# Second branch product of a hybrid encoder block as seven half products, with its sums formed earlier

## The chip, the cores and the metric

The kernel runs on one core of a Trainium2 chip. The metric is device time in microseconds (us); the time before is a median of three runs. All arithmetic is fp32: a product of two fp32 matrices is made of three TensorE matmuls on high and low parts (high x high, high x low, low x high), which the code calls fp32r parts.

## The reference

One encoder block on x of 1024 tokens by 1024 channels:

```
h = rms_norm(x);  proj = h @ w_in      (q, k, v, r, gate codes, attention q/k/v, two branch gates)
A = gated linear attention(proj) @ w_o_gla        (branch A)
B = windowed attention(proj)     @ w_o_swa        (branch B)
x = x + (sigmoid(gate_a) * A + sigmoid(gate_b) * B) @ w_out
x = x + (silu(h2 @ w_g) * (h2 @ w_u)) @ w_ffn_out,   h2 = rms_norm(x)
```

The change is about `B`'s projection, a product of a 1024 x 1024 weight (`w_ob` in the kernel) with the attention's output.

## The kernel before

Activations stand transposed: channels on the 128 partitions, tokens along the free dimension in two halves of 512 (`HT`). The stages follow each other on TensorE:

1. the first projections and the norm (0 to about 40 us);
2. the linear attention, 46 slots (loop over `t`, L649 to L656). Each slot issues pieces of the linear attention and, between them, a share of the dense projections' matmuls (`fill`, table `GF`). Behind each slot one step of `x_sums` (L606) runs: a load of a tile of x, or a difference of two such tiles that is stored to DRAM, for the later pair products. These tiles come from the pool `xn`, three buffers of 128 x 512;
3. the windowed attention, 22 slots (L865 to L880), filled in the same way from the dense projections. Head outputs are stored to DRAM by `a_out` (L820), one store for each of four heads, 64 KB each;
4. the other halves of three projections as pairs (`pair_*`, to about 720 us);
5. branch A's projection by `seven` (L1123);
6. branch B's projection by `both` (L1096);
7. `w_out` by `seven` again, then the feed-forward part.

`seven` multiplies 2 x 2 blocks with seven half products in place of eight. The row tiles of the weight are taken as pairs (k, k + 4), the contraction as its two halves, the tokens as two halves. The half products are named "11", "21", "T1", "T2", "T3", "T4", "22"; the T products take sums of weight blocks (formed by VectorE when needed, `comb` and `sub`) and differences of operand blocks. Each is done for four k, each time 4 blocks x 3 matmuls of 128 x 512 (`product`, L910). `both` does the plain product: for each of 8 row tiles `m`, two weight units of 4 blocks, and 6 matmuls a block (two token halves, three part products).

A weight tile is loaded (`rawload`, `wunit`), its high part copied by ScalarE and its low part subtracted by VectorE (`wsplit`, L890), into pools of five buffers each (`wh`, `wl`). Operand tiles are split in the same way into named sets (`xset`, sets S0 to S6, each with four high and four low tiles). A gate is loaded from DRAM, put through a sigmoid on ScalarE, and multiplied with the product and added by VectorE (L1269, L1270). `merge` (L1188) then forms the operands of the `w_out` product.

Order: TensorE's order is the written one (`manual_schedule`). For the other engines a scheduler fixes the order at compile time by program priority and a timing model; `tc.keep_in_program_order` and `tc.issue_after` pin single instructions. All DMA transfers are issued by SyncE, in order: one that waits for a buffer or for data holds up those behind it. On-chip memory is given out in pools stacked on each other; when a group of pools is closed (`glas.close()` L657, `swas.close()` L881), a pool that is laid over one of them waits for that pool's last use. The pools `swc` and `swt` hold the windowed attention; `tp` and `bo`, which follow, lie over `swt` (`tp` holds the tiles t2h, t2l, np, nt; `bo` the sets S0 to S3, used from about 600 us on), and `wq` (wr2, ws) lies over `swc` alone.

## Time and profile before

| | |
|---|---|
| median of three runs | 1606.47 us (1606.43 to 1606.72) |
| profiled execution | 1607.29 us, span 1605.5 us, granted TensorE clock 1.00 |
| TensorE matmul busy | 1596.9 us, 7532 matmuls |
| VectorE / ScalarE busy | 1209.1 us / 903.5 us |
| DMA | 323.24 MB, mean 201 GB/s |

A page of the profile gives the busy time of each engine (PE is TensorE, PEld its weight loads, DVE VectorE, ACT ScalarE, SP SyncE, SPq SyncE's queue), the chain of work that ended last, groups of instructions (line, engine, operation, output <- inputs with buffer numbers left out, then busy us, mean ns of one, idle us before them and what ended it), and the DMA issues (KB each, median us to landing). Stretches give the busy time of each engine between two times. Matmuls are pipelined, so their listed lengths overlap; the distance between starts is what counts. A line number can be a helper's.

### The profile page before, as it was taken

What the parts mean: (1) busy time and instruction counts of PE and PEld (TensorE: products, weight loads), DVE (VectorE), ACT (ScalarE), POOL (GpSimd) and SP (SyncE); (2) the same over time, 40 slices, a digit from 0 to 9 for tenths busy, and PEclk for the clock granted to TensorE, in tenths of its full rate; (3) what the DMA queues carried; (4) which work ended last, traced back from release to release, by engine and by line L of the source; (5) the groups of instructions that cost most, each with busy time, mean ns of one, the idle gap of its engine ahead of it and who ended that gap; (6) DMA issues with size and microseconds to landing.
All of it is one profiled execution on the core that took longest, in us unless ns stands there. A gap on an engine that the chain in (4) does not pass through costs nothing.

```text
span 1605.5 us, 23093 instructions
## 1 busy us (share of the span) xinstructions
PE 1596.9 (99%) x7532; PEld 1330.1 (83%) x7532; DVE 1209.1 (75%) x2287; ACT 903.5 (56%) x1859; POOL 0.2 (0%) x4
## 2 busy tenths in 40 slices
PE   9999999999999999999999999999999999999999
PEld 6888888888888788888888888888888888888887
DVE  8568888746999678786855877777777878689655
ACT  7456778755998645455633656844444444354442
POOL 0000000000000000000000000000000000000000
PEclk9999999999999999999999999999999999999999
DMA  8856767888544487868733656634344564695433
GB/s 270 301 196 213 248 216 259 285 264 286 173 145 139 152 291 246 273 228 273 243 124 105 220 186 204 202 114 151 112 145 157 191 202 161 207 330 175 151 99 118
DMA packets 197979, 323.24 MB, mean 201 GB/s; under 512 B 23423, under 2 KB 49919, under 8 KB 197858
## 3 DMA queue, kind: packets, MB, share of 16 engines
q1 hardware_dynamic: 197858, 321.77, 60.8%
q8 instruction: 59, 0.97, 0.2%
q14 instruction: 62, 0.51, 0.1%
HBM read 216.29 MB, written 105.39 MB: 200 GB/s over the span
## 4 chain that ended last, share of the span: by engine, by line
PE 95%; DVE 2%; ACT 1%; DMA 1%; issue 0%; SPq 0%; DVEq 0%; ACTq 0%
PE mm L73 22%; PE mm L916 10%; PE mm L915 10%; PE mm L914 10%; PE ch L73 8%; PE mm L1458 7%; PE ch L1458 6%; PE ch L914 5%; PE ch L916 5%; PE ch L915 5%; PE mm L246 4%; PE ch L813 1%; PE ch L585 0%; PE ch L756 0%; PE ch L490 0%
## 5 line engine op out<-in xcount | busy, mean ns | idle before, releaser
L893 ACT ACTIVATE wh<-ws 128x512 fp32r<-128x512 f32 x164 | 103.2, 630 | 157.4 <-PE mm L915 83.8
L73 PE MATMUL mm<-wh,xl 128*128 128x512 f32 x320 | 127.3, 398 | 0.0
L73 PE MATMUL mm<-wh,xh 128*128 128x512 f32 x320 | 126.9, 397 | 0.3 <-ACT lrt L313 0.3
L73 PE MATMUL mm<-wl,xh 128*128 128x512 f32 x320 | 127.1, 397 | 0.0
L894 DVE TENSOR_TENSOR wl<-ws,wh 128x512 fp32r<-128x512 f32 x164 | 112.2, 686 | 15.8 <-ACT wh L893 15.4
L67 ACT ACTIVATE wh<-wr 128x512 fp32r<-128x512 f32 x114 | 71.1, 630 | 55.2 <-issue 16.9
L69 DVE TENSOR_TENSOR wl<-wr,wh 128x512 fp32r<-128x512 f32 x114 | 77.9, 686 | 22.0 <-ACT wh L67 20.5
L893 ACT ACTIVATE wh<-a 128x512 fp32r<-128x512 f32 x66 | 41.6, 632 | 90.3 <-PE mm L1458 42.7
L893 ACT ACTIVATE wh<-wr 128x512 fp32r<-128x512 f32 x76 | 47.9, 631 | 60.9 <-PE mm L915 20.2
L894 DVE TENSOR_TENSOR wl<-a,wh 128x512 fp32r<-128x512 f32 x66 | 45.5, 690 | 40.4 <-ACT wh L893 40.2
L73 PEld LDWEIGHTS mm<-wh,xh 128*128 128x128 f32 x320 | 60.3, 188 | 10.6 <-ACT lrt L313 0.8
L1458 PE MATMUL mm<-hl,wh 128*128 128x512 f32 x176 | 68.6, 390 | 0.0
L1458 PE MATMUL mm<-hh,wl 128*128 128x512 f32 x176 | 68.6, 390 | 0.0
L1458 PE MATMUL mm<-hh,wh 128*128 128x512 f32 x176 | 68.5, 389 | 0.0
L73 PEld LDWEIGHTS mm<-wl,xh 128*128 128x128 f32 x320 | 60.3, 188 | 9.6
L73 PEld LDWEIGHTS mm<-wh,xl 128*128 128x128 f32 x320 | 60.3, 188 | 9.0
L907 DVE TENSOR_TENSOR ws<-wr,wr 128x512 f32<-128x512 f32 x80 | 54.5, 686 | 8.0 <-DMA wr<-in_w_f_dram 4.0
L894 DVE TENSOR_TENSOR wl<-wr,wh 128x512 fp32r<-128x512 f32 x76 | 51.9, 684 | 7.6 <-ACT wh L893 7.0
L1425 DVE TENSOR_TENSOR hl<-hr,hh 128x512 fp32r<-128x512 f32 x77 | 52.8, 686 | 5.1 <-ACT hh L1424 5.1
L1424 ACT ACTIVATE hh<-hr 128x512 fp32r<-128x512 f32 x77 | 47.6, 619 | 7.9 <-DMA hr<-B 4.1
L1458 PE MATMUL ch<-hh,wh 128*128 128x512 f32 x132 | 51.4, 389 | 0.0
L1458 PE MATMUL ch<-hh,wl 128*128 128x512 f32 x132 | 51.4, 389 | 0.0
(449 smaller groups left out, 4910.1 us busy)
## 6 DMA issues: line engine op xcount, KB each, us to landing
wr<-in_w_fi_dram SPq DMA_DIRECT2D x110, 256.0 KB, 4.0
wr<-in_w_f_dram SPq DMA_DIRECT2D x96, 256.0 KB, 3.7
wh<-wh SPq DMA_DIRECT2D x80, 256.0 KB, 3.3
wl<-wl SPq DMA_DIRECT2D x80, 256.0 KB, 3.1
B<-c SPq DMA_DIRECT2D x44, 256.0 KB, 2.1
T<-st SPq DMA_DIRECT2D x44, 256.0 KB, 3.1
a<-in_w_fo_dram SPq DMA_DIRECT2D x44, 256.0 KB, 5.1
hr<-T SPq DMA_DIRECT2D x44, 256.0 KB, 2.7
```

Source lines behind the costliest of these rows:

```text
L67: nc.scalar.activation(h, raw, AF.Copy)
L69: nc.vector.tensor_tensor(l, raw, h.bitcast(F32), op=ALU.subtract)
L73: nc.tensor.matmul(o, a, b, start=start, stop=stop)
L246: nc.tensor.matmul(Y[q], w[:, c], x, start=f0, stop=f1, skip_group_check=True)
L893: nc.scalar.activation(h, src, AF.Copy)
L894: nc.vector.tensor_tensor(l, src, h.bitcast(F32), op=ALU.subtract)
L907: nc.vector.tensor_tensor(t, x, y, op=op)
L914: nc.tensor.matmul(o, h[:, c], x[kk][0], start=start and kk == 0, stop=False, skip_group_check=True)
L915: nc.tensor.matmul(o, h[:, c], x[kk][1], start=False, stop=False, skip_group_check=True)
L916: nc.tensor.matmul(o, l[:, c], x[kk][0], start=False, stop=kk == nk - 1, skip_group_check=True)
L1425: nc.vector.tensor_tensor(l, r, h.bitcast(F32), op=ALU.subtract)
L1458: nc.tensor.matmul(ys[m], a[:, c], b, start=f0, stop=f1, skip_group_check=True)
```

## The change

- `both`, `prep_b` and `merge` go. Branch B's product is done by a new function `branch_b` with the same seven half products as `seven`, for the first time with branch B's operands and weights. Its results are added to the sum in five gated parts (`gated_by`), 20 in all.
- The operand sums (T1 to T4) of branch B are formed by `b_sums(n)`, called behind the last four slots of the windowed attention. It loads four blocks from DRAM, takes four differences and stores them. It uses the two buffers of `qr`. The head outputs go into grouped DRAM tiles with one store of 256 KB for four heads.
- The weight sums for T1, T2 and T3, and the ready-made high and low parts of the sum for "22", are formed by `w_sums` behind `x_sums` in the linear attention (24 more steps; slots 2 to 13 take two steps), and stored. So are the parts of `w_out`'s first four weight tiles, which the next `seven` then reads (`first`).
- While branch A's product runs, three operand sets of four tiles are loaded and split (`bset`) in place of four such sets; the other four sets follow during `branch_b`. The operands of the `w_out` product are formed in the last steps of `branch_b` and the first of `seven` (`m_T1`, `m_rest`).

```
+        def w_sums():
...
+            def form(key, d, x, y, op):
+                tc.keep_in_program_order(nc.vector.tensor_tensor(d, x, y, op=op))
+                if key:
+                    put(key, d)
+
+            def parts(key, d):
+                h, l = (gtile(t, (P, 512), FR, bufs=1) for t in ("pwh", "pwl"))
+                nc.scalar.activation(h, d, AF.Copy)
+                tc.keep_in_program_order(nc.vector.tensor_tensor(l, d, h.bitcast(F32), op=ALU.subtract))
+                for n, v in (("h", h), ("l", l)):
+                    put((key[0] + n, key[1]), v.bitcast(F32))
+
+            w = i["w_ob"]
+            for k in range(4):
+                a, c, b = load(w[k, 0]), load(w[k + 4, 1]), load(w[k + 4, 0])
+                form(("bs1", k), c, b, c, ALU.add)
+                yield
+                form(("bs3", k), b, a, b, ALU.subtract)
+                yield
+                form(("bs2", k), c, c, a, ALU.subtract)
+                yield
+                d = load(w[k, 1])
+                form(None, d, d, c, ALU.subtract)
+                yield
+                parts(("bs4", k), d)
+                yield
+                parts(("wo", k), load(i["w_out"][k, 0]))
+                yield
...
-                if t:
+                for _ in range(2 if 2 <= t <= 13 else t > 0):
                     next(sums, None)
...
-            for h in range(4):
-                nc.sync.dma_start(out=scr["b", 4 * g + h, n // 4][:, (n % 4) * P:(n % 4 + 1) * P],
-                                  in_=ob[:, h])
+            nc.sync.dma_start(out=heads(f"b{g + 1}{n // 4 + 1}", n), in_=ob)
+
+        def b_sums(n):
+            x1, x2 = (sw.tile([P, 8, P], F32, tag="qr", name=nm("qr")) for _ in range(2))
+            a, b, c, d = x1[:, 0:4], x1[:, 4:8], x2[:, 0:4], x2[:, 4:8]
+            for q, v in (("b11", a), ("b12", b), ("b22", c), ("b21", d)):
+                nc.sync.dma_start(out=v, in_=heads(q, n))
+            for q, t, x, y in (("bT1", b, b, a), ("bT2", c, c, b), ("bT3", a, c, a), ("bT4", d, d, c)):
+                nc.vector.tensor_tensor(t, x, y, op=ALU.subtract)
+                nc.sync.dma_start(out=heads(q, n), in_=t)
...
+                    b_sums(t - 2 * KT - 2)
...
+        def parted(key, k):
+            r = []
+            for n in "hl":
+                t = wp.tile([P, 512], FR, tag="w" + n, name=nm("w" + n), bufs=5)
+                nc.sync.dma_start(out=t.bitcast(F32), in_=scr[key + n, k])
+                r.append(t)
+            return r
...
+        def gated_by(d, v, m, s):
+            turns[0] += 1
+            g = bt.tile([P, HT], F32, tag=("ga", "gb")[turns[0] % 2], name=nm("gb"))
+            nc.sync.dma_start(out=g, in_=scr[f"gb{m}", s])
+            nc.scalar.activation(g, g, AF.Sigmoid)
+            nc.vector.tensor_tensor(g, v, g, op=ALU.mult)
+            nc.vector.tensor_tensor(d, g, d, op=ALU.add)
+
+        def branch_b(w, S, mid):
...
+            for k in K:
+                Y[k] = mmtile()
+                product(Y[k], load(w[k, 0]), S["11"], 4, True, True)
+                X[k] = chtile((P, HT))
+                nc.scalar.copy(X[k], Y[k])
+                after("11", k)
+            for k in K:
+                product(Y[k], load(w[k, 1]), S["21"], 4, False, True)
+                gated_by(xg[k][0], Y[k], k, 0)
+                after("21", k)
+            for k in K:
+                Z[k] = mmtile()
+                product(Z[k], load(scr["bs1", k]), S["T1"], 4, True, False)
+                p5[k] = bo.tile([P, HT], F32, tag=f"S3h{k}", name=nm("p5"))
+                nc.scalar.copy(p5[k], Z[k])
+                after("T1", k)
+            for k in K:
+                product(X[k], load(scr["bs2", k]), S["T2"], 4, False, True)
+                gated_by(xg[k][1], X[k], k, 1)
+                after("T2", k)
+            for k in K:
+                product(X[k], load(scr["bs3", k]), S["T3"], 4, False, True)
+                nc.vector.tensor_tensor(p5[k], X[k], p5[k], op=ALU.add)
+                gated_by(xg[k + 4][1], p5[k], k + 4, 1)
+                after("T3", k)
+            for k in K:
+                product(X[k], load(w[k + 4, 1]), S["T4"], 4, False, True)
+                gated_by(xg[k + 4][0], X[k], k + 4, 0)
+                after("T4", k)
+            for k in K:
+                product(Z[k], parted("bs4", k), S["22"], 4, False, True)
+                gated_by(xg[k][1], Z[k], k, 1)
+                after("22", k)
...
-                   2: (lambda k: prep_b(0, k), lambda k: prep_b(1, k)), 3: (lambda k: prep_b(2, k),),
-                   6: (lambda k: prep_b(3, k),)}, hl)
+                   2: (bset("11"),), 3: (bset("21"),), 6: (bset("T1"),)}, hl)
+            branch_b(i["w_ob"], BX, {"11": (bset("T2"),), "21": (bset("T3"),),
+                                     "T1": (bset("T4"), lambda k: yset("11", k, xg[k][0])), "T2": (bset("22"),),
+                                     "T4": (lambda k: yset("21", k, xg[k + 4][0]),), "22": (m_T1,)})
...
-            for m in (0, 4, 1, 5, 2, 6, 3, 7):
-                g = [gate(f"gb{m}", s) for s in range(2)]
-                y = both(i["w_ob"], m, ob)
-                for s in range(2):
-                    nc.vector.tensor_tensor(g[s], y[s], g[s], op=ALU.mult)
-                    nc.vector.tensor_tensor(xg[m][s], g[s], xg[m][s], op=ALU.add)
-                if m > 3:
-                    merge(m - 4)
...
-                  {0: (lambda k: yset("T3", k, xg[k][0]), lambda k: yset("22", k, xg[k + 4][1])),
-                   1: (lambda k: yset("T2", k, xg[k][1]),),
+                  {0: (m_rest,), 1: (lambda k: yset("T2", k, xg[k][1]), lambda k: yset("T3", k, xg[k + 4][1])),
...
+                  None, lambda k: parted("wo", k))
```

`bset(q)` loads the four tiles of an operand set from DRAM and splits them into a set of S0 to S6; `first` in `seven` replaces the split weight of its first half product.

More of the change, by code (lines that the diff above doesn't have):

```diff
@@ L1145, in seven @@
                 Y[k] = mmtile()
-                product(Y[k], wsplit(held(k, k, 0), 512), S["11"], 4, True, True)
+                product(Y[k], first(k) if first else wsplit(held(k, k, 0), 512), S["11"], 4, True, True)
                 X[k] = chtile((P, HT))
@@ L1186, in seven, with load, after @@
                 after(6, k)
-        def merge(k):
+        turns = [0]
+        def gated_by(d, v, m, s):
[6 more added lines that the diff above has]
+        def branch_b(w, S, mid):
+            K = range(4)
+            n = [0]
+            def load(src):
+                n[0] += 1
+                return wsplit(rawload(src, n[0] % 2), 512)
+            def after(q, k):
+                for f in mid.get(q, ()):
+                    f(k)
+            Y, X, Z, p5 = ([None] * 4 for _ in range(4))
+            for k in K:
[31 more added lines that the diff above has]
+                after("22", k)
```

68 lines of the change are left out of this document (34 added, 34 removed).

## The prediction

> **What bounds the kernel now.** I read the page first: the busy shares and the chain that ended last.
>
> ```profile
> span 1605.5 us, 23093 instructions
> ...
> PE 1596.9 (99%) x7532; PEld 1330.1 (83%) x7532; DVE 1209.1 (75%) x2287; ACT 903.5 (56%) x1859; POOL 0.2 (0%) x4
> ...
> PE 95%; DVE 2%; ACT 1%; DMA 1%; issue 0%; SPq 0%; DVEq 0%; ACTq 0%
> ```
>
> TensorE carries the end: 95% of the chain, and 8.6 us without work in the whole span (1605.5 - 1596.9). A removed matmul is worth its full length wherever the other engines keep up. Next I took the chain in order of time (start, length, what), for the stage that changes and its neighbours:
>
> ```profile
> 352.57 20.21 PE mm L73 x89
> ...
> 554.62 14.53 PE mm L246 x64
> ...
> 808.77 87.04 PE mm L73 x384
> ```
>
> The last row is the second branch product: 384 matmuls without a break in 87.04 us, so 87.04 / 384 = 0.2267 us each. Last, the busy times by stretches, to see which engine has room where the change puts new work:
>
> ```profile
> core 0: us, PE busy (x) PEld busy (x) DVE busy (x) ACT busy (x) POOL busy (x), PEclk, DMA share, GB/s
> 70.00:150.00 80.00, 80.00 (x427) 68.60 (x427) 57.80 (x118) 41.70 (x97) 0.00 (x0) 1.00 0.63 211
> 230.00:300.00 70.00, 69.61 (x408) 60.44 (x408) 61.68 (x149) 57.65 (x163) 0.00 (x0) 1.00 0.78 259
> 300.00:350.00 50.00, 49.38 (x263) 41.16 (x264) 24.06 (x65) 34.76 (x104) 0.00 (x0) 1.00 0.83 276
> 370.00:380.00 10.00, 10.00 (x49) 8.26 (x48) 3.68 (x10) 1.87 (x5) 0.00 (x0) 1.00 1.03 373
> 380.00:520.00 140.00, 139.32 (x758) 120.09 (x757) 132.54 (x381) 127.60 (x313) 0.00 (x0) 1.00 0.54 169
> 528.00:555.00 27.00, 25.92 (x134) 20.60 (x133) 16.30 (x42) 18.18 (x45) 0.00 (x0) 1.00 0.38 127
> 540.00:550.00 10.00, 9.02 (x46) 6.68 (x45) 5.17 (x13) 7.92 (x20) 0.00 (x0) 1.00 0.38 116
> 809.00:896.00 87.00, 87.00 (x385) 72.07 (x385) 51.63 (x83) 33.85 (x59) 0.00 (x0) 1.00 0.37 113
> 896.00:985.00 89.00, 89.00 (x395) 73.66 (x394) 72.77 (x117) 51.50 (x89) 0.00 (x0) 1.00 0.66 211
> ```
>
> From 555 to the end TensorE never waits in the product stages. It loses about a microsecond at the attention's end (25.92 of 27) and about one around the end of the linear attention (0.39 and 0.62). Those two places are where the change adds work.
>
> **The product (a term of the sum).** Before: 8 output tiles x 2 weight units x 4 blocks x 6 matmuls = 384. After: 7 half products x 4 row tiles x 4 blocks x 3 matmuls = 336. The 48 that go, of the same shape, are 48 x 0.2267 = 10.88 us off the path; the stage becomes 76.2 us.
>
> **Does VectorE keep up there?** I counted the instructions in the new stage: 24 subtractions for weight low parts, 40 for the gates (20 gatings of a product and an addition), 16 for the splits of four operands, 4 additions of the held product, 12 splits for the next product and 4 differences: 100 on VectorE, and 24 + 20 + 8 + 16 + 12 = 80 on ScalarE.
>
> ```profile
> L1269 DVE TENSOR_TENSOR gb<-mm,gb 128x512 f32<-128x512 f32 x15 | 9.7, 686 | 26.7 <-PE mm L73 26.7
> L67 ACT ACTIVATE wh<-wr 128x512 fp32r<-128x512 f32 x14 | 8.6, 623 | 20.7 <-issue 16.9 <-PE mm L73 3.7
> L837 DVE TENSOR_TENSOR S4l<-xg,S4h 128x512 fp32r<-128x512 f32 x4 | 2.8, 688 | 0.0
> ```
>
> ```profile
> 360.30 0.68 DVE L679 TENSOR_TENSOR qA<-cosb,qg 128x512 f32<-128x512 f32 x1
> 360.90 0.69 DVE L680 SCALAR_TENSOR_TENSOR qB<-sinb,qg 128x512 f32<-128x512 f32 x1
> 361.51 0.69 DVE L681 TENSOR_TENSOR qB<-sinb,qg 128x512 f32<-128x512 f32 x1
> ```
>
> In these groups of the stage (busy, mean ns, then idle before) one VectorE instruction of 512 columns takes 0.686 us, but in the row of three from the timeline each starts 0.60 us after the last: their ends overlap. So 100 are 60 to 69 us, and 80 on ScalarE at 0.623 are 50 us, both inside 76.2. Step by step, a product gives TensorE 12 x 0.2267 = 2.72 us, and the fullest steps hold four VectorE instructions: 2.4 to 2.75 us. The last four products and the first four of the next stage read ready-made weight parts and cost VectorE none. The stage at 896 to 985 is nearly this one (seven half products, gates replaced by residuals): VectorE 72.77 of 89, TensorE 89.00 of 89. No gain beyond the matmuls is possible, since TensorE waits nowhere here. I take 0, with 0 to 1 us as bounds; the cover is the five weight buffers, prepared up to four products (10.9 us) ahead.
>
> The stage before it splits 12 operands instead of 16, so it gets lighter. Transfers in the new stage: 24 weights, 8 parts, 20 gates, 16 operands of 256 KB, 17.8 MB in 76 us or 234 GB/s, against 259 and more in stretches where TensorE is full. Nothing.
>
> **Sums of weights in the linear attention.** 24 steps are added behind the 32 that exist, and slots 2 to 13 now take two. Each new step has one VectorE instruction, 8 have a ScalarE copy, and together they issue 20 loads and 28 stores of 256 KB. The existing steps, by the view of their tile (min/median/max ns, first and last start), the last output of the linear attention, by the timeline, and two rows of transfers (KB, median us to landing):
>
> ```profile
> L603 DVE TENSOR_TENSOR xn<-xn,xn x16: 682/685/689, 78.0 to 303.3; 128x512 f32<-128x512 f32 x16
> ```
>
> ```profile
> 352.61 0.37 ACT L587 COPY ot<-ch 128x256 f32<-128x256 f32 x1 [1.01 <-PE ch L585]
> ```
>
> ```profile
> xT<-xn SPq DMA_DIRECT2D x16, 256.0 KB, 2.8
> qr<-sq SPq DMA_DIRECT2D x16, 256.0 KB, 3.2
> ```
>
> The third old step ran at 78.0 and the last, slot 32, at 303.3; the last slots end near 352.6. Doubling in slots 2 to 13 falls roughly into 70 to 150, where VectorE has 57.8 of 80: 12 x 0.6 us fit. Slots 21 to 32 only exchange one step for another; VectorE is at 88% there (61.68 of 70) and gets no instruction more. Slots 33 to 44 get 12 new VectorE instructions in 46 us where it is half idle (24.06 of 50). What is tight there is the transfers: 24 x 256 KB = 6.3 MB in 46 us is 137 GB/s on top of 276, together 413, and the highest rate of any stretch I read is 373. (413 - 373) x 46 us = 1.8 MB, or 4.9 us, would be left over. All transfers go through SyncE's queue in order, so the dense projections' weights stand behind the new loads, and the new loads wait for one of three staging buffers.
>
> ```profile
> SPq L170 <- PE mm L73: 23.1, 18, 3.9
> ```
>
> The wait of that queue for TensorE (23.1 us in 18 waits) says that the re-read weights are fetched as early as the five buffers allow, up to 10.9 us of matmuls ahead of use. That covers a lag of 4.9 us for weights; the short backward chain of the linear attention has less cover. Bounds 0 and 4.9 us; I take 1, near the 0.62 already lost in that stretch.
>
> **Operand sums at the attention's end.** Four rounds, one a slot, each four loads, four dependent subtractions, four stores; 16 VectorE instructions x 0.6 = 9.6 us, of which 528 to 555 leaves 10.7 free (16.30 of 27). On SyncE the 64 stores of the attention's outputs become 16, against 32 issues more in the rounds. The rounds borrow the two query buffers, and the memory of the whole attention is handed to the next stage at its last use. The timeline shows such a hand-over, and the tile view of np (us to landing) and its copy what follows it:
>
> ```profile
> 357.21 0.69 DVE L678 TENSOR_TENSOR kA<-cosb,kg 128x512 f32<-128x512 f32 x1 [7.48 <-DMA o<-ot]
> ...
> 528.95 0.60 PE L756 MATMUL ch<-ident,qr 128*128 128x128 f32 x4
> ...
> 555.14 0.64 ACT L836 ACTIVATE t2h<-xn 128x512 fp32r<-128x512 f32 x1
> ...
> 574.43 0.39 PE L914 MATMUL mm<-t2h,wh 128*128 128x512 f32 x1
> ```
>
> ```profile
> L935 ACT COPY mm<-np x12: 578/591/603, 557.8 to 686.7; 128x512 f32<-128x512 f32 x12
> ...
> DMA to landing us min/median/max: 2.6/3.5/6.5
> ```
>
> The attention's first table (kA) waited 7.48 us for the store of another tile (ot), the last user of the old memory. Likewise the first tile of the next stage (t2h) started at 555.14, right behind the attention's last matmuls. After the change it waits for the fourth round's stores. The second query buffer is free at 529.3 (528.95 and the transposes behind it). A round is a load of 3.2, three subtractions behind the last load 1.8, a store of 2.8 and under one for queues: 8.5 us. Four end near 563.3. The next stage then loads np (3.5) and copies it (0.59), ready at 567.4; the fourth t2 split, which waits for a staging buffer, is ready near 569.5. TensorE wants them at 574.43 and 2.0 later, and works through 64 dense matmuls in between. Free of cost then, unless a round takes over 10.2 us. Beside that, four new instructions can push into the softmax chain, which already holds TensorE up (9.02 of 10). Bounds 0 and 5.0; I take 1.
>
> **Hand-over after the linear attention.** Its memory now ends with two stores of weight parts in slot 44. If they land 5 us after 357.2, the first keys still come in time, for the 20.21 us row of 89 matmuls stands before their transposes. Nothing.
>
> **Sum.** The profiled execution took 1607.29 us, 1.79 around its span of 1605.5, and 0.82 over the median of 1606.47. 1607.29 - 10.88 + 1 + 1 = 1598.41; less 0.82, 1597.6 us.
>
> **Rivals.** (A) The rounds hold the memory too long. For: each round waits for a load and a store to land, and single loads took up to 6.5 (np). Against: 7 us of cover (574.43 - 567.4). At 11.5 us a round the memory is free at 575.3, np is copied at 579.4, and TensorE waits 5.0 us: 1606.47 - 10.88 + 1 + 5.0 = 1601.6. The trace's clock is 1.00 in each stretch above, even in 540 to 550, where TensorE idles longest, and no row shows what a wait of 5 us does. The Trainium skill (TensorE: Matmul & The Clock Gate, Part 1) says that about 3.4 us without matmuls halve the clock until about 3.4 us of work have passed; by that rule A would cost some 1.7 us more, an estimate, and end at 1603.3.
>
> (B) Transfers at the linear attention's end lag by the full 4.9: 1606.47 - 10.88 + 4.9 + 1 = 1601.5. For: 413 wanted against 373. Against: stores may lag freely.
>
> (C) Slower: VectorE's fixed order in the new stage. Its multiplication must wait for the end of a product; what stands behind it waits too, the low parts of later weights among them. If those stood behind the multiplication of the product just before their own, every gated product would cost TensorE 3 x 0.686 = 2.06 us. It decides at 10.88 / 20 = 0.54 us a product; half of the 20 would give 1606.47 - 10.88 + 20.6 = 1616.2. For it: the multiplication row waits 26.7 us for TensorE already. Against: the same pattern at 896 to 985 costs nothing.
>
> (D) A and B together: 1606.47 - 10.88 + 4.9 + 5.0 = 1605.5, no change. That the change does not remove the matmuls cannot be: the count follows from its loops.
>
> **Chances.** Forecast (1595.3 to 1599.6) 0.66; B 0.13; A 0.10; D 0.06; C 0.05. Low end: all hidden, and 0.3 less of today's waits, 1595.3. High end: over A and B and a little, 1602. A measurement of this kernel tells 0.2% (3.2 us) from no change: forecast, A and B are faster, 0.89, less 0.02 for an A whose wait passes 6.7 us (1603.3): 0.87; D and those 0.02 are no change, 0.08; C is slower, 0.05.
>
> **What would show it.** One row of 336 matmuls in 76.2 us; TensorE full from 555 to 985 apart from A; the first t2h at about 563; VectorE near 62 us busy in the new stage; stretch 300 to 350 above 350 GB/s with about a microsecond lost. A TensorE gap of over 3 us at 574 makes A right, several in 300 to 350 B, and gaps between products of the new stage C.

## The result and the profile after

The changed kernel takes 1643.08 us (median of four runs, 1641.65 to 1643.71) against 1606.60 for the kernel before (four runs, 1606.43 to 1607.35). The ratio is 1.0225 (95% interval 1.0207 to 1.0243): 36.5 us slower. The forecast was 1597.6, with 1595.3 to 1602.0 as its range; sign and size are both wrong.

First the page of the changed kernel: span, busy times, and the chain of waits by engine.

```profile
span 1641.3 us, 23247 instructions
...
PE 1604.9 (98%) x7484; PEld 1328.0 (81%) x7484; DVE 1249.7 (76%) x2355; ACT 922.7 (56%) x1895; POOL 0.2 (0%) x4
...
PE 78%; DVE 7%; DMA 6%; ACT 5%; issue 2%; SPq 1%; ACTq 0%; DVEq 0%
```

The 48 matmuls are gone (7484 for 7532), yet TensorE is listed as busy for 8.0 us longer, and its share of the chain falls from 95% to 78%. The next step is to find where in the kernel the time goes. For that I matched the TensorE instructions of the two traces in order and subtracted their starts. The table shows how much each part of the kernel has lost (plus) or gained (minus) against the kernel before; the limits of the parts are times of the kernel before. The same measure is used for every kernel further down.

| kernel | up to 385: linear attention | 385 to 544: attention | 544 to 584: its end | 584 to 990: products | 990 to end |
|---|---|---|---|---|---|
| changed | 23.2 | 1.2 | 15.4 | -8.0 | 3.8 |

Of the 23.2 us, 0.2 are lost by 222, 2.7 from there to 331, and 20.3 between 331 and 385. Stretches of the changed kernel with the places of loss and with the new product (846 to 925) follow (columns as before: start and end, length, busy time and count of PE, PEld, DVE, ACT, POOL, granted clock, DMA share, GB/s):

```profile
300.00:350.00 50.00, 45.05 (x234) 37.01 (x233) 27.63 (x66) 34.06 (x97) 0.00 (x0) 0.97 0.82 276
334.00:386.00 52.00, 40.36 (x159) 30.06 (x159) 20.61 (x53) 21.09 (x61) 0.00 (x0) 0.87 0.84 273
590.00:622.00 32.00, 23.71 (x88) 17.67 (x87) 22.29 (x36) 15.15 (x28) 0.00 (x0) 0.84 0.94 299
846.00:925.00 79.00, 78.19 (x345) 64.42 (x344) 60.28 (x96) 41.81 (x75) 0.00 (x0) 1.00 0.71 226
```

In 334 to 386 TensorE has only 40.36 us of 52, and the granted clock is 0.87, where it was 1.00. That is one reason why "busy" grew while matmuls went: a matmul issued at half clock takes 0.43 us in this trace, where one at full clock takes 0.23. In 300 to 350 as a whole the transfers run at 276 GB/s, which is what they ran at before and far from the 413 that the forecast feared.

How the linear attention's end stalls is seen in a few rows of the timeline of all engines (start, length, engine, line; in brackets the idle time before and what ended it):

```profile
334.95 0.39 PE L73 MATMUL mm<-wh,xh 128*128 128x512 f32 x1
...
336.89 0.91 ACT L579 ACTIVATE ob<-ob,ors 128x256 f32<-128x256 f32 x2 [0.24 <-DVE ors L101]
...
337.45 0.44 PE L585 MATMUL ch<-ident,ob 128*128 128x128 f32 x2 [2.11 <-ACT ob L579]
...
341.69 0.42 DVE L566 TENSOR_TENSOR ob<-ob,ch 128x256 f32<-128x256 f32 x1 [4.32 <-PE ch L73]
...
345.13 0.61 ACT L67 ACTIVATE wh<-wr 128x512 fp32r<-128x512 f32 x1
...
345.79 0.50 PE L73 MATMUL mm<-wh,xh 128*128 128x512 f32 x1 [2.17 <-ACT wh L67]
```

It is a ring. TensorE waits for ScalarE (ob), VectorE then waits 4.32 us for TensorE, and the copy of the next dense weight (wh, L67) stands on ScalarE behind all that, until 345.13; SyncE's next store, at 345.77, waits for the same copy. TensorE stops again, for 2.17 us, for a weight whose raw tile had landed by 341.2. No engine here is short of capacity: VectorE has 20.61 us of work in those 52.

These two stops are the smaller part. Of the 11.3 us that TensorE stands still between 331 and 386 in stops over 0.3 us, 7.0 are waits for dense weights that were split before and are read again from DRAM (wh<-wh, wl<-wl). Below are two rows of the waits in 326 to 400 (waiter, releaser, us, times, longest) and three of the timeline ahead of the longest stop there, in which TensorE has one matmul between 372.4 and 378.2:

```profile
PE mm L73 <- DMA wh<-wh: 5.0, 3, 3.2
...
PE mm L73 <- DMA wl<-wl: 2.5, 3, 1.8
```

```profile
372.69 0.63 ACT L639 ACTIVATE pwh<-xn 128x512 fp32r<-128x512 f32 x1 [3.67 <-DMA xn<-in_w_out_dram]
...
374.07 0.32 SPq L116 DMA_DIRECT2D wol<-pwl  x1
374.44 0.45 SPq L170 DMA_DIRECT2D wl<-wl  x1
```

A step of the weights' sums waits for its load, its split follows on ScalarE and VectorE, its store waits on SyncE for the split, and the load of the dense weight that TensorE needs next (L170) is issued right behind that store. It lands at 378.15, and TensorE goes on at 378.19.

At the attention's end the chain of waits of the changed kernel (start, length, what) goes through the last round of operand sums. Two rows of tile views give the start of the first load of the rounds and of the first t2h (behind the durations: first and last start), and two rows of the waits in 555 to 612 give what TensorE stands still for:

```profile
588.64 5.17 DMA qr<-b
...
595.46 0.68 DVE qr L881
...
601.28 0.43 SPq L986
...
601.75 0.43 SPq L955
...
602.23 4.64 DMA wr<-in_w_f_dram
...
606.96 0.70 DVE ws L960
...
607.69 0.64 ACT wh L946
...
608.37 0.80 PE ch L967
```

```profile
L879 SPq DMA_DIRECT2D qr<-b x14: 524/644/1102, 553.9 to 589.4; - x14
```

```profile
L888 ACT ACTIVATE t2h<-xn x4: 616/624/633, 599.5 to 604.4; 128x512 fp32r<-128x512 f32 x4
```

```profile
PE ch L967 <- ACT wh L946: 7.7, 2, 6.7
...
PE ch L73 <- DVE pl L862: 3.1, 2, 2.9
```

Four rounds take from 553.9 to 599.5, or 11.4 us each. The weight tile that TensorE wants at 601.7 is issued at 602.23, behind loads for the memory that was just handed over (L986 loads np), and TensorE stands still for 6.7 us. An earlier stop of 2.9 us, until 572.1, is the softmax chain: its step pl stands on VectorE behind differences of a round whose load took 5.6 us to land. Last comes a wait that the forecast does not have, at the start of the feed-forward's last product: SyncE's queue in the kernel before, and in the changed one (waiter, releaser, us, times, longest):

```profile
SPq L1433 <- PE mm L916: 4.3, 1, 4.3
```

```profile
SPq L1530 <- PE ch L969: 7.7, 1, 7.7
```

The first load of w_ffn_out goes into memory that was held by operand sets of the product before it. In the changed kernel another half product is the last reader of that memory (its sums lie in ch in place of mm), one product of 12 matmuls or 2.7 us later.

### The profile page after: what moved, and what is told of

It reads as the page before. It is cut to its first block, busy times and chain, and to the rows that moved or that the text cites. A ratio compares the mean times of both kernels' runs of the same rounds, so it can differ in the third digit from the quotient of the medians.

```text
span 1641.3 us, 23247 instructions
## 1 busy us (share of the span) xinstructions
PE 1604.9 (98%) x7484; PEld 1328.0 (81%) x7484; DVE 1249.7 (76%) x2355; ACT 922.7 (56%) x1895; POOL 0.2 (0%) x4
## 4 chain that ended last, share of the span: by engine, by line
PE 78%; DVE 7%; DMA 6%; ACT 5%; issue 2%; SPq 1%; ACTq 0%; DVEq 0%
PE mm L73 12%; PE mm L967 9%; PE mm L969 9%; PE mm L968 9%; PE mm L1555 7%; PE ch L1555 5%; PE ch L969 5%; PE ch L967 5%; PE ch L968 5%; PE ch L73 5%; PE mm L246 2%; DMA wl<-wl 1%; DMA qr<-b 1%; DMA ga<-ga 1%; DVE xg L1046 1%
## 5 line engine op out<-in xcount | busy, mean ns | idle before, releaser
L69 DVE TENSOR_TENSOR wl<-wr,wh 128x512 fp32r<-128x512 f32 x98 | 66.7, 686 | 16.7 <-ACT wh L67 16.5
L67 ACT ACTIVATE wh<-wr 128x512 fp32r<-128x512 f32 x98 | 61.0, 630 | 27.8 <-PE mm L73 16.4
L969 PE MATMUL ch<-S6h,wl 128*128 128x512 f32 x136 | 53.0, 390 | 0.1
L969 PE MATMUL mm<-S0h,wl 128*128 128x512 f32 x136 | 52.9, 389 | 0.0
L967 PE MATMUL ch<-S6h,wh 128*128 128x512 f32 x136 | 52.9, 389 | 0.0
```

The source lines that it names most:

```text
L67: nc.scalar.activation(h, raw, AF.Copy)
L69: nc.vector.tensor_tensor(l, raw, h.bitcast(F32), op=ALU.subtract)
L967: nc.tensor.matmul(o, h[:, c], x[kk][0], start=start and kk == 0, stop=False, skip_group_check=True)
L969: nc.tensor.matmul(o, l[:, c], x[kk][0], start=False, stop=kk == nk - 1, skip_group_check=True)
```

## The experiments

My theory after the profile is that the change loses through waits, not through work: the steps that load, combine and store stand in the fixed orders of SyncE, VectorE and ScalarE, and what TensorE needs stands behind them. The rivals are too many bytes (rate), too many instructions (engines), and memory handed over late. All losses below are in the parts of the table above, each kernel against the trace of before; "time" is the median of its runs, and "ratio" compares them with runs of the kernel before on the same chip. The kernels with waits scatter by 2 to 9 us from run to run (e11 from 1610.4 to 1619.1), and the parts come from one traced run each, so a difference of a few us between the same part of two kernels is weak evidence. The traced runs of e10 and e8 are the fastest of their four, 5.4 and 4.1 us under the median. Kernels e1, e2, e3, e6, e10 and e11 leave work out and compute other values; they show what a part costs.

| kernel | time | ratio (95%) | to 385 | to 544 | to 584 | to 990 | to end |
|---|---|---|---|---|---|---|---|
| no weights' sums (e1) | 1621.6 | 1.0071 to 1.0101 | 1.3 | 0.7 | 12.2 | -4.7 | 5.7 |
| no rounds (e2) | 1630.2 | 1.0121 to 1.0154 | 25.6 | 0.2 | -1.3 | -5.7 | 3.9 |
| neither (e3) | 1609.0 | 0.9998 to 1.0017 | 0.1 | -0.3 | 0.0 | -0.9 | 2.5 |
| other queue (e4) | 1696.5 | 1.0539 to 1.0570 | 18.8 | 10.9 | 59.1 | -4.2 | 3.2 |
| loads ahead (e5) | 1640.4 | 1.0194 to 1.0225 | 21.3 | 0.6 | 14.0 | -6.2 | 3.7 |
| same bytes (e6) | 1618.1 | 1.0056 to 1.0086 | 0.3 | 0.7 | 14.2 | -8.0 | 2.5 |
| no transfers (e10) | 1623.5 | 1.0079 to 1.0116 | -1.3 | 1.4 | 11.8 | -5.5 | 4.3 |
| rounds later (e7) | 1638.0 | 1.0177 to 1.0211 | 23.9 | 2.1 | -1.6 | 1.9 | 3.8 |
| free stores (e11) | 1614.8 | 1.0030 to 1.0063 | 11.4 | 0.7 | -1.1 | -7.8 | 3.5 |
| stores apart (e13) | 1642.2 | 1.0202 to 1.0245 | 24.2 | 1.6 | 10.9 | -6.2 | 3.8 |
| all in place (e8) | 1622.3 | 1.0072 to 1.0105 | 0.7 | -0.1 | 0.0 | 7.1 | 2.9 |
| two a slot (e15) | 1638.9 | 1.0176 to 1.0207 | 15.8 | 1.5 | 14.8 | -6.1 | 3.7 |
| rounds staged (e17) | 1662.6 | 1.0326 to 1.0357 | 25.9 | 0.7 | 29.5 | -4.6 | 4.7 |
| no parts (e18) | 1631.5 | 1.0128 to 1.0162 | 6.4 | 1.4 | 15.5 | -5.1 | 5.9 |
| idle engine (e19) | 1642.5 | 1.0200 to 1.0231 | 27.6 | 1.0 | 13.3 | -5.3 | 0.4 |
| spread (e20) | 1639.2 | 1.0177 to 1.0211 | 28.8 | -0.2 | 0.0 | 3.3 | -0.2 |
| weights first (e21) | 1640.9 | 1.0187 to 1.0221 | 26.2 | 1.5 | 13.5 | -6.9 | -0.1 |

### Which part of the change loses

The first three leave out one part or both; in e1 and e3 the branch product splits plain weights, as `load(w[k + 4, 0])` in place of `load(scr["bs1", k])`.

```
-            yield from w_sums()
...
-                    b_sums(t - 2 * KT - 2)
```

> Left out: the sums of weights and the ready-made parts; the branch product reads plain weight blocks in their place and splits them itself, so its values are others. If the 23.2 us that the changed kernel has lost by the time 385 us of the kernel before (20.3 of them between 331 and 385) come from the steps of weights' sums, this kernel is 23 us faster than the changed one, near 1620. If they come from the other layout of the attention's stores or from code around it, it stays near 1640.

> Left out: the four rounds that form the operand sums at the attention's end; the branch product reads plain blocks for them, so its values are others. If the 15.4 us that the changed kernel loses between 544 and 584 us (times of the kernel before) come from the rounds, it is 13 to 15 us faster than the changed one, near 1629, with the loss in the linear attention unchanged. If the memory handed over late has another cause, it stays near 1640.

> Left out: both the sums of weights and the operand sums; the branch product is seven half products of plain blocks. The prediction's 10.88 us less in the product stage should then be alone: 1606.5 - 10.9 = 1595.6 if nothing else is lost; 1602 if the 1.1 us in the new stage, the 1.8 behind it and the 3.8 at the start of the last product belong to the new product stage itself and not to the sums.

The first two came out as said: without the weights' sums the loss up to 385 is 1.3 instead of 23.2, without the rounds the attention's end loses nothing. The two losses hardly touch each other. The third is the surprise: with both gone the product does not show its 10.9 us, and the time is that of the kernel before. The stages from 584 to 990 gain 0.9, and the start of the last product loses 2.5. In that kernel's new stage (a stretch, and from its waits in 775 to 930: waiter, releaser, us, times, longest) the rows are:

```profile
803.00:880.00 77.00, 73.94 (x325) 60.60 (x324) 58.01 (x94) 43.85 (x78) 0.00 (x0) 1.00 0.65 198
```

```profile
ACT gb L1239 <- DMA gb<-gb: 18.3, 13, 4.7
...
DVE wl L945 <- ACT wh L944: 8.7, 9, 2.5
PEld mm L967 <- DVE wl L945: 4.9, 3, 1.8
...
PEld mm L965 <- ACT ch L1260: 3.9, 2, 3.1
```

VectorE is busy 58 of 77 us and ScalarE 44, and TensorE still loses 3 us there and more on both sides. ScalarE stands 18.3 us at gates that have not landed, and copies that TensorE needs (ch, wh) come late; that they are late because they stand behind the gates is read from these rows and was not tested.

### The linear attention

Four theories for the 23.2 us: the rate, the engines' work, SyncE's queue (a store that waits for its difference holds up the weights behind it), and loads that land too late for VectorE's fixed order. Moving all of it, and the rounds, to GpSimd's queue came first:

```
-                nc.sync.dma_start(out=t, in_=src)
+                nc.gpsimd.dma_start(out=t, in_=src)
```

> Complete computation. All loads and stores of the weights' sums and of the rounds are issued by GpSimd's queue, which is otherwise idle, in place of SyncE's; bytes, VectorE and ScalarE work and places stay. Theory of the queue (a store that waits for its difference, which waits for its own load, holds up the weights behind it on SyncE): most of the 20.3 us in the linear attention's end goes and part of the 15.4 at the attention's end, 1606 to 1620. Theory of the rate (too many bytes for the DMA engines there): the gaps stay, 1635 to 1645.

Neither theory foresaw 53 us more than the changed kernel takes. 18.8 are lost up to 385 and 59.1 at the attention's end, where GpSimd's queue itself is the slow part (from its waits in 540 to 660):

```profile
DVE qr L886 <- DMA qr<-b: 47.8, 8, 15.1
POOL qr L884 <- issue: 36.4, 13, 3.6
```

That queue takes 36.4 / 13 = 2.8 us to issue a load, without a wait that the profile shows, and VectorE stands 47.8 us behind the loads. So this kernel tests the new queue more than the theories. The next three take the coupling apart. In e5 every load moves like this one:

```
                form(("bs2", k), c, c, a, ALU.subtract)
+               d = load(w[k, 1])
                yield
-               d = load(w[k, 1])
                form(None, d, d, c, ALU.subtract)
```

In e6 the work goes and the transfers stay, in e10 the other way round:

```
-               tc.keep_in_program_order(nc.vector.tensor_tensor(d, x, y, op=op))
...
-                   put(key, d)
+                   put(key, cosb.rearrange("p a b -> p (a b)"))
```

```
-               nc.sync.dma_start(out=t, in_=src)
...
-               tc.keep_in_program_order(nc.vector.tensor_tensor(d, x, y, op=op))
-               if key:
-                   put(key, d)
+               tc.keep_in_program_order(nc.vector.tensor_tensor(d, flat(cosb), flat(sinb), op=op))
```

> Complete computation; each load of the weights' sums is issued one step (one slot) ahead of the difference that uses it. Theory of the queue (stores that wait for differences which wait for their own loads hold up the dense weights on SyncE): the loss up to 385 us (23.2 us in the changed kernel) falls below 8, total near 1628. Theory of the rate (too many bytes) and theory of the engines' order (the added VectorE and ScalarE instructions push the copies of the dense weights behind the backward chain): no change, near 1640.

> Left out: every difference, copy and split of the weights' sums; their 20 loads and 28 stores stay, the stores taken from a resident table, so that no transfer waits for an engine's work. The branch product's values are others. Theory of the rate: the loss up to 385 us stays near 23 us, total near 1640. Theories of the queue's waits and of the engines' order: it goes to under 5, near 1620.

> Left out: every load and store of the weights' sums; their VectorE and ScalarE instructions stay, on resident tables, with the same pins. The branch product reads plain weight blocks. Theory of the engines' order: the loss up to 385 us stays near 20, total near 1640. Theories of the rate and of the queue: under 3, near 1620.

The transfers alone lose 0.3 us and the instructions alone nothing in the traced run (the other three runs of e10 are 5 to 7 us longer, and no trace says where). A stretch that holds the linear attention's end, of the kernel with the transfers and of the one with the instructions, has TensorE full:

```profile
331.00:386.00 55.00, 54.96 (x263) 45.11 (x261) 26.57 (x72) 25.66 (x71) 0.00 (x0) 1.00 0.86 282
```

```profile
331.00:386.00 55.00, 54.96 (x265) 45.32 (x265) 29.59 (x77) 25.05 (x67) 0.00 (x0) 1.00 0.87 288
```

Rate and engines' work, each by itself, are far from 23.2 us: both rivals fall. What costs is the dependence of one on the other. A load issued a slot earlier changes little (21.3). That does not clear the loads: in e5 too TensorE's longest stop in that part, 4.2 us, is for re-read weights, behind stores and loads of the sums in SyncE's queue. Three more look at the stores and at the place.

The edits of e11 (the parts and the rounds are changed in the same way), e13 and e15 are:

```
-                   put(key, d)
+                   put(key, flat(cosb))
```

```
+            def put(key, t):
+                d = scratch("_".join(map(str, key)))
+                nc.gpsimd.dma_start(out=d, in_=t)
```

```
-                for _ in range(2 if 2 <= t <= 13 else t > 0):
+                for _ in range(2 if t >= 2 else t > 0):
```

> Left out: what is stored. The loads and the VectorE and ScalarE work of the weights' sums stay as in the changed kernel, on the loaded tiles, but the stores are taken from a resident table, so no store waits for an engine; in the rounds at the attention's end the differences are left out too and the stores are taken from the table. Same bytes throughout. Theory of the queue (stores that wait for results hold SyncE): the 20.3 us between 331 and 385 fall under 4. Theory of the late loads (VectorE and ScalarE, in their fixed order, stand at a difference whose load has not landed): the 20 us stay. At the attention's end: waits, under 3 of the 15.4 stay; rate, 12 or more stay.

> Complete computation; only the 28 stores of the weights' sums go through GpSimd's queue, loads stay where they are on SyncE. Theory of the queue: the 20.3 us between 331 and 385 fall under 6, total near 1628. Theory of the late loads: about 20 stay, total near 1640. The attention's end is untouched and keeps 12 to 15.

> Complete computation; two steps in every slot from the second on, so that the weights' sums are over by about slot 29 and slots 33 to 45 hold none. If the loss belongs to the place (the short backward chain of the last slots), the 23.2 us lost up to 385 fall under 8, total near 1626. If it belongs to the coupling of load, difference and store wherever it stands, 15 to 23 us are lost earlier, total near 1640.

Free of waiting stores the last part (331 to 385) loses 4.4 instead of 20.3, a little over what I had set as the limit. So most of the last part hangs on the stores; over the whole linear attention it is half, for this kernel loses 7.0 before 331 where the changed one loses 2.9. With the stores on another queue SyncE is freed and nothing is won in all (24.2), so the theory that SyncE's queue alone is the cause falls. It does not clear SyncE's queue in the changed kernel, whose longest stop in this part goes through it, as shown above; the stores on GpSimd's queue bring losses of their own. 9.4 us are lost before 331 and 14.8 in the last part, and the store of one low part (bs4l) took 6.8 us to land, where no low part's store took over 3.0 in the changed kernel. A tile is held until its store has landed, and the waits of that kernel (326 to 405) show GpSimd's stores waiting for differences, and VectorE waiting for a store:

```profile
POOL bs L629 <- DVE xn L638: 17.7, 4, 9.8
...
DVE pwl L645 <- DMA bs4l<-pwl: 8.9, 2, 4.7
```

In e13 VectorE, pinned to its order, waits 8.9 us for the store of the split before. In the changed kernel no split waits for that. Two steps a slot (e15) move the loss with the steps: nothing is lost after 331, and 15.8 before. So the loss belongs to the coupling, not to the place. The next kernel leaves out the parts, which have a single buffer each for high and low:

```
-               form(None, d, d, c, ALU.subtract)
+               form(("bs4", k), d, d, c, ALU.subtract)
                yield
-               parts(("bs4", k), d)
                yield
-               parts(("wo", k), load(i["w_out"][k, 0]))
                yield
```

> Complete computation; the ready-made parts go: the sum for the last half product is stored as it is and split in the branch product's stage, and so are the first weights of the next product. 16 loads and 16 stores stay of 20 and 28, and the two single buffers with them are gone; the remaining steps keep their slots. If the single buffers (a split that waits for the store of the one before) are the cause, the 20.3 us between 331 and 385 fall under 6, total near 1630. If the store of each difference on SyncE is the cause, 10 or more stay. The new stage has 8 VectorE instructions more and may lose 2 to 4 us by them.

The loss up to 385 is 6.4 instead of 23.2, 5.6 of it in the last part. The eight steps of ready-made parts were nearly three quarters of the loss; 16 loads and 16 stores stay. The limit set for the single buffers is met, but the kernel takes away the steps' copies, splits and 16 stores together with the buffers, and the changed kernel's profile has no wait for such a buffer. What it shows is SyncE waiting at the steps' stores, 5.0 us for differences alone between 222 and 400. No run gave the parts a second pair of buffers. The last kernel puts the whole of it on an engine that has nothing else to do:

> Complete computation; all of the weights' sums, their loads, differences, copies, splits and stores run on GpSimd and its queue, in the same slots. Also, in another place, the operand sets of the feed-forward product are handed out anew, so that the set of its half product 22 lies outside the memory that the last product's loads take over. Theory of the coupling (each store, difference and load of a sum waits in the fixed order of SyncE, VectorE and ScalarE, whose other work TensorE needs): the 23.2 us lost up to 385 fall under 3. If the sums' steps load memory or the transfers as such, over 10 stay. At 1391, memory handed over one half product (2.7 us) later than before: the 3.8 us there fall under 1; order of the engines: they stay. Total 1616 to 1620 with both.

```
-               tc.keep_in_program_order(nc.vector.tensor_tensor(d, x, y, op=op))
+               nc.gpsimd.tensor_tensor(d, x, y, op=op)
...
-       HOMEX = {"11": 0, "T1": 6, "22": 2, "T2": 1, "T3": 3, "21": 5, "T4": 4}
+       HOMEX = {"11": 0, "T1": 2, "22": 4, "T2": 1, "T3": 3, "21": 5, "T4": 6}
```

The first half is a miss: 27.6 us are lost up to 385. They are lost elsewhere, all of them by 331 and nothing after. GpSimd was not held to the slots and formed all sums and splits between 227 and 332 of its own trace, where the changed kernel takes until 374. Here are the same two VectorE groups in 230 to 330 in the kernel before, and in this one while GpSimd works (busy us, mean ns):

```profile
L69 DVE TENSOR_TENSOR wl<-wr,wh 128x512 fp32r<-128x512 f32 x22 | 15.1, 686 | 5.0 <-ACT wh L67 5.0
L556 DVE SCALAR_TENSOR_TENSOR tlb<-kb,decb,thb 128x256 fp32r<-128x256 f32 x13 | 6.2, 480 | 0.2 <-ACT thb L555 0.2
```

```profile
L69 DVE TENSOR_TENSOR wl<-wr,wh 128x512 fp32r<-128x512 f32 x16 | 14.6, 910 | 0.4 <-ACT wh L67 0.4
L556 DVE SCALAR_TENSOR_TENSOR tlb<-kb,decb,thb 128x256 fp32r<-128x256 f32 x10 | 8.4, 835 | 0.0
```

These VectorE instructions become a third to three quarters longer beside GpSimd's, while others keep their length (L566, ob<-ob,ch: 415 and 409 ns; L558, kb: 483 and 477). How much of the 27.6 us comes from that is not shown, and this kernel doesn't tell whether the coupling would vanish on a truly separate engine. The second half came out as said: with the operand sets handed out anew, the 3.8 us at the start of the last product are 0.4, and -0.2 and -0.1 in the two later kernels that have the same edit.

### The attention's end

That bytes are not the cause is shown by e11 above, which keeps all loads and stores of the rounds, leaves out their differences, and loses -1.1 there. The next kernel asks whether it is the place:

```
-            x1, x2 = (sw.tile([P, 8, P], F32, tag="qr", name=nm("qr")) for _ in range(2))
+            a, b, c, d = (stage((P, 4, P)) for _ in range(4))
...
                     pair_T4(f)
+                if j < 8:
+                    b_sums(j // 2)
```

> Complete computation; the four rounds of operand sums run between the first five pairs of the pair products (about 630 to 720 us) in the four staging buffers, in place of the attention's end. If the 15.4 us lost between 544 and 584 us come from where the rounds stand (weights queued behind their stores, memory handed over late), it is 13 to 15 us faster than the changed kernel, near 1629, like the kernel without rounds. If the rounds cost what they cost anywhere, TensorE waits among the pairs instead and it stays near 1640.

The attention's end is free (-1.6), but the pairs, which lost nothing in any other kernel, now lose 11.3 (584 to 745). From the waits of that kernel in 640 to 790:

```profile
PE mm L965 <- DVE st L974: 3.5, 2, 2.0
```

TensorE waits for the sum (st) of the pair before, which stands on VectorE behind differences of the round and waits there for a round's store to free a staging buffer. So the rounds cost time in both places, though not the same: 11.3 us here, about two thirds of the 16.7 that lie between e2 and the changed kernel at the attention's end. Two kernels try to part the memory from the queue at the old place: the rounds in the staging buffers (first hunk above alone), and np loaded behind the weights:

```
+            g.r11, g.r21 = rawload(i["w_f"][a, 0], True), rawload(i["w_f"][b, 0], True)
+            g.s = comb(g.r21, rawload(i["w_f"][b, 1], False), ALU.add)
+            g.w = wsplit(g.s, 512)
             p1 = tp.tile([P, HT], F32, tag="np", name=nm("np"), bufs=2)
             nc.sync.dma_start(out=p1, in_=scr[f"{nme}{m}", "p1"])
...
-            g.r11, g.r21 = rawload(i["w_f"][a, 0], True), rawload(i["w_f"][b, 0], True)
-            g.s = comb(g.r21, rawload(i["w_f"][b, 1], False), ALU.add)
-            g.w = wsplit(g.s, 512)
```

> Complete computation; the four rounds stand where they stand, but in the four staging buffers, which are not handed over, in place of the query buffers. If the 15.4 us between 544 and 584 come from the memory handed over late, they fall under 4, total near 1630. If they come from SyncE's queue (the weights and np behind the rounds' stores), 12 or more stay, total near 1641.

> Complete computation; two edits in separate places. Each pair product loads its weights ahead of the first-half tile np that goes into the handed-over memory (in the changed kernel the weights stand behind np on SyncE, and np waits for the rounds' last store): if it is np's place in the queue, the 12.5 us between 564 and 584 fall to 6 or less; if the rounds' transfers as a whole are late, they stay over 10. The operand sets of the feed-forward product are handed out so that the half product 22 reads memory that is not handed over: the 3.8 us at 1391 fall under 1. Total 1631 to 1634 with both, 1639 with the second alone.

The first is no test of it: the staging buffers are those of the dense projections, and 29.5 us are lost, 23.9 of them in this wait (550 to 660):

```profile
PE mm L246 <- DVE st L249: 23.9, 3, 13.7
```

The second moved np away and kept 13.5 of 15.4: np's place in the queue is not the cause. In its chain TensorE's weights wait for the sum ws on VectorE, which now stands behind the splits of t2, whose loads wait for the same memory. Memory and order are tied to each other here, and their shares stay open.

### The product without sums made ahead

> Complete computation; the weights' sums are formed in the branch product's stage as the other two products of seven do, the operands' differences while branch A's product runs; the two places of the changed kernel that lose time are as in the kernel before. 20 VectorE instructions more in the stage and 16 in the one ahead of it. If only the placing of the sums lost time, it is 1596 to 1600. If the fixed order in the new stage also costs (the kernel with neither sums lost 10 us there), 1602 to 1612.

> Complete computation; as the kernel with the idle engine, and the rounds at the attention's end go too: each operand difference is formed when its set is split, one VectorE difference more a step in branch A's and the new stage. If nothing but the placing of the sums was wrong, the product's 10.9 us show less about 3 lost in the fixed order of the new stage: 1597 to 1601. If the differences in the product stages cost as much as the kernel with all sums in place lost there, 1606 to 1612.

In e8 the weights' sums are formed by `comb` and `sub` in the new stage, and T1 to T4 of the operands in the step "T3" of branch A's product; in e20 one operand difference a step is formed when its set is split:

```
+                sub(sm[k], sm[k], raw(w[k, 0]))
+                product(X[k], wsplit(sm[k], 512), S["T2"], 4, False, True)
...
+            sub(t, t, u)
+            BX[q].append(xset(HOMEB[q], k, t))
```

Both came out beyond the bad end of what was expected: 1622.3 against 1602 to 1612, and 1639.2 against 1606 to 1612, though 28.8 us of e20's loss lie ahead of the attention, in the weights' sums on GpSimd that it shares with e19. The stages from 584 to 990 lose 7.1 and 3.3 us in place of gaining 10.9, so 18 and 14 us go there. One place in e20 shows how (VectorE's timeline):

```profile
929.51 2.49 DVE L1050 TENSOR_TENSOR xg<-xg,xg 128x512 f32<-128x512 f32 x4
931.92 0.69 DVE L894 TENSOR_TENSOR S4l<-xg,S4h 128x512 fp32r<-128x512 f32 x1
932.52 3.69 DVE L1050 TENSOR_TENSOR xg<-xg,xg 128x512 f32<-128x512 f32 x6
936.13 0.68 DVE L951 TENSOR_TENSOR wl<-wr,wh 128x512 fp32r<-128x512 f32 x1
```

Ten differences of `m_rest`, which are needed three steps later, stand in VectorE's fixed order ahead of the low part that TensorE needs now; it stands still from 932.5 to 936.9. No kernel here beats the kernel before; of those that compute all of the output, the one with the sums in place (1622.3) comes nearest.

## Why the prediction was wrong

- **The product, -10.88.** The matmuls are gone as counted. The stages around gain 8.0 in the changed kernel, and between 0.9 and 8.0 in kernels with the same half products and no operand differences in these stages, so 3 to 10 us go there. The step that failed is the answer that VectorE keeps up ("I take 0, with 0 to 1 us as bounds"). The load was right (60.28 us in 79, forecast 60 to 69); the inference from load to time was not. The kind of mechanism is rival C's, an engine's fixed order, but the place is another: C had VectorE's multiplication waiting for the end of a product, which is 3.6 us of the waits in 846 to 945 of the changed kernel, while in the longest row there ScalarE stands 20.0 us at gates that have not landed. The size is a seventh to a half of C's 20.6 us, and 18 in e8. What the gates alone cost was not tested.
- **Weights' sums: took 1, bounds 0 to 4.9; measured 23.2.** The step that failed is the price by counts, 12 instructions in a half-idle engine and 6.3 MB over a top rate: transfers and instructions are each nearly free by themselves (e6, e10). What costs is the chain of a step: its store stands on SyncE until a load has landed and two engines in fixed order have worked, and the dense weights stand behind it. So the cover that the forecast claimed, weights fetched up to 10.9 us ahead, was gone: SyncE waits for TensorE to free a weight buffer for 11.9 us between 222 and 400 before, and for 3.1 in the changed kernel. Part of the loss is also the copy of a landed weight, which stood on ScalarE behind the backward chain. Slots 2 to 13 were right (0.2 us lost by 222). Rival B had the place, and weights behind the new loads on SyncE, but the wrong reason for the lag, the rate.
- **Operand sums: took 1, bounds 0 to 5; measured 15.4.** This is rival A: it was to decide at 10.2 us a round, and a round took 11.4. The step that failed first is the sum for a round, 8.5: loads of a round took 5.17 (the chain's first row above) and 5.6 us to land where I had put 3.2, and the stores stand in SyncE's queue between other transfers, which "under one for queues" priced. Then its size: A had 5.0 for TensorE's wait, and the stop that ends at 608.37 lasts 6.7 us with half clock after it. The stop in the softmax chain that ends at 572.1 (2.9) and two that end at 594.4 and 598.4 (0.6 and 1.0) come on top. The forecast named the softmax chain, and took 1 us for the whole place.
- **The half clock.** The forecast could show no row for it. Now there is one, and it matters: of some 20 us lost from 334 to 408, 14.5 are in steps of over 0.6 us from one matmul to the next, and 4.8 in matmuls issued at half clock; of some 12 from 590 to 622, 8.8 and 3.1.
- **Hand-over after the linear attention: nothing.** This held in the changed kernel. The first table waited 3.0 us for the store of a part and stood at 377, as late as all around it, and TensorE has no stop over 0.3 us between 378.2 and 408.
- **Start of the last product: not in the forecast; 3.8.** The diff renumbers the operand sets (`HOMEX`), and I took that for bookkeeping. Undoing it takes the loss away in e19, e20 and e21.
- **The rivals.** A and B together was rival D, at 1605.5 and 0.06. The places were right; the prices of A and B were too small by a factor of three to five.

What stays open: whether the parts cost through their stores' place on SyncE or through ScalarE's and VectorE's order; how the 6.4 us that are left without the parts divide between buffers and orders; whether the coupling would be free on an engine that doesn't slow VectorE; memory against order at the attention's end; and the cause of the 3 to 10 us lost around the new product.

## What to carry to other kernels

A background step that loads, combines and stores is to be priced by its chain: follow it from the load to the landed store through every engine and queue of fixed order, and ask what stands behind it at each. Free bytes and free instructions do not make it free (0.3 and -1.3 us alone, 23.2 together). How far more buffers would help was not tested here. An engine that is busy three quarters of a stage has room, but not at the moment that counts: ask what each added instruction will stand in front of. When a diff renumbers buffers, look for who reads the handed-over memory last.

## What the runs showed of the hardware

The granted clock falls after short stops. Stretches of the changed kernel around the gap of 601.3 to 608.4, and two quarters of a microsecond around the gap of 334.95 to 337.45:

```profile
602.00:604.00 2.00, 0.00 (x0) 0.00 (x0) 0.09 (x1) 0.89 (x2) 0.00 (x0) 1.00 0.91 210
604.00:606.00 2.00, 0.00 (x0) 0.00 (x0) 0.69 (x1) 1.03 (x2) 0.00 (x0) 0.57 1.04 345
606.00:608.00 2.00, 0.00 (x0) 0.00 (x0) 1.04 (x2) 0.49 (x2) 0.00 (x0) 0.50 1.04 389
...
614.00:615.00 1.00, 1.00 (x5) 0.81 (x4) 1.00 (x2) 1.00 (x3) 0.00 (x0) 0.74 0.83 227
```

```profile
338.00:338.25 0.25, 0.25 (x2) 0.21 (x1) 0.00 (x0) 0.25 (x1) 0.00 (x0) 0.58 1.00 353
...
341.25:341.50 0.25, 0.25 (x4) 0.25 (x3) 0.00 (x0) 0.00 (x0) 0.00 (x0) 0.59 0.96 322
```

In the first case it falls near 604.3, 2.6 us after the last matmul, and is back at 614.5, 6.1 us after matmuls had resumed. In the second a stop of 2.1 us (335.3 to 337.4) was enough, and the clock fell only after TensorE had resumed, for 3.4 us (338.0 to 341.5).

The clock records of the traces give a pattern. In the changed kernel the clock falls at 338.0, 355.1, 375.6, 573.6 and 604.3, whole multiples of 3.41 us apart, and stays low for 3.41, 3.41, 6.83, 3.41 and 10.24 us. Taken over the eighteen traces of the changed kernel and the experiments, on this grid of 3.41 us: the half clock followed every full-clock window in which TensorE stood still for 2.0 us or more and none with under 1.39 (between these, some), and the full clock came back only after windows with at most 0.63 us of standing still. So a short stop costs or not by where it falls on the grid, and one low window full of matmuls costs about half of itself, 1.7 us, an estimate from the 0.43 and 0.23 us a matmul above. The Trainium skill (TensorE: Matmul & The Clock Gate, Part 1) gives about 3.4 us of idleness, and about as much of work until the clock is back, counted in windows that run freely; the halving and the windows agree with these traces, but a stop well under 3.4 us did cost here.

GpSimd at work slows some of VectorE's instructions: 686 to 910 ns and 480 to 835 ns in the rows shown for e19, while L566 (415 and 409) and L558 (483 and 477) kept their length. Its queue is slow for the rounds' tiles of 512-byte rows, at 2.8 us to issue a load in e4.
